# Gate and up products of an FFN in Strassen's seven-product block form, tokens in quarters

## The chip, the cores and the metric

The kernel runs on one core of a Trainium2 chip. The metric is device time in microseconds of one execution. A core has five engines that run their own instruction queues side by side: TensorE (PE, matrix products into PSUM banks), VectorE (DVE), ScalarE (ACT), GpSimd (POOL) and SyncE (SP, which here issues the DMA transfers). They wait for one another through semaphores. The weights of a matmul are loaded by a separate instruction (PEld in the profile) that overlaps the matmul before it.

## The reference

One inference step of one layer for 1,024 prompt tokens and 32 sample tokens (T = 1,056), model width D = 1,024:

```python
proj = x @ w_in                       # 4096 columns: HGRN2 heads and retention heads
o_h, o_r = hgrn2_chunkwise(...), retention_chunkwise(...)   # each head-normalised and gated
x = layer_norm(alpha * x + concat(o_h, o_r) @ w_out)
hidden = silu(x @ w_gate) * (x @ w_up)                      # FF = 2816 columns
x = layer_norm(alpha * x + hidden @ w_down)
```

All of it is in fp32; the outputs are x and the two heads' states. The change concerns the last two lines, with the normalisation ahead of them and the product with `w_out`.

## The kernel before

Features lie on the partitions and tokens along the free axis, so every product is "weights 128x128 times tokens". fp32 accuracy is had by splitting each operand into a rounded part (hi, type fp32r) and the remainder (lo): a product is three matmuls into one PSUM bank, hi·hi, hi·lo and lo·hi (`group`, the matmul in L224). `split` makes the two parts: ACT casts (L187), and DVE or POOL subtracts (L188). `load_w` (L191) has SP fetch a raw 128x1024 tile `wr` (two buffers) and splits it, mostly on POOL, into full hi and lo tiles `wh`/`wl` or `xh`/`xl` (three buffers each).

The order of the work: the program is written as one stream of large products. Beside it stands a queue `side` of generators (normalisation `norm`, mixer steps, centring `center`), and `tick(rate)` after each piece of the stream takes `rate` steps out of it. The tile framework's scheduler then fixes each engine's own order by priorities (`high_priority` moves work ahead).

The phases are: the mixer with the input projection (to about 489 us); the product with `w_out` (`oproj`, L774); and the FFN (L841 on). Tokens come in three chunks of 400, 400 and 256 (`CHB`). `oproj` runs chunk by chunk over eight output tiles m, adding to `Y` (x with its mean over the features taken out: `xload` L757, `xsub` L766 and L768). After each chunk, `norm` squares Y on ACT and adds the squares on DVE and POOL (L685), gets the sum over features and the reciprocal root (`rstd`, matmul L665, Newton steps L213–L217), spreads it over the partitions (`spread`, matmul L656), multiplies Y by it on DVE (L706) and POOL (L704), applies gain and bias on ACT (L707), and splits the result into `X`, the FFN's operand.

The FFN goes through 11 pairs of FF tiles (22 tiles of 128 columns). For each tile and chunk `gu` (L797) makes one full product with `w_gate` and one with `w_up` over all eight k tiles, then silu (ACT, L808), multiplication (DVE, L809) and a split of the hidden tile into `hh` and `hl`. `down` (L812, matmul L822) adds a pair's product with `w_down` into Y on DVE (L834 and L836); the `down` of pair p is issued inside pair p+1, after its first gate and up products, so hidden tiles are long finished by then. In the last pair `down` follows chunk by chunk, and the final `norm` of each chunk with it; `norm_tail` (L736) ends the program. Late in the FFN `center` (POOL, L728 and L733) takes the running mean out of Y, and the last weights of `w_down` are centred.

PSUM has eight banks: in this phase three under the name `pj` and five under `mx`.

Of the kernel before, what the change touches and what calls it, by code (L numbers as in the profile page):

```python
# [9 lines left out]
F32 = mybir.dt.float32  # L10
# [6 lines left out]
P = 128  # L17
# [18 lines left out]
RF = 2.0  # L36
CHB = [(0, 400), (400, 400), (800, 256)]
CBM = 400
# [4 lines left out]
WE = (3, 4, 5)  # L43
TV = (6, 7)
PJ = 3
NH = 5
LP1 = 0
# [16 lines left out]
# columns of the shape-only constants  # L64
# [3 lines left out]
def _consts():  # L68
    parts = []
    off = 0  # L70

    def put(name, a):
        nonlocal off
        a = np.asarray(a, np.float64).reshape(P, -1)
        _CI[name] = (off, a.shape[1])
        off += a.shape[1]
        parts.append(a)
# [29 lines left out]
    cst = np.concatenate(parts, 1).astype(np.float32)  # L107
# [13 lines left out]
    return cst, masks.reshape(P, -1), cs.astype(np.float32)  # L121


_CST, _MASKS, _CS = _consts()


def body(tc, ctx, a):
# [19 lines left out]
    masks = const.tile([P, len(SMALL), 16], U8, name="masks")  # L147
# [4 lines left out]

    def K_(name):
        o, n = _CI[name]
        return cst[:, o:o + n]
# [5 lines left out]
    # work of the mixer and of the norms, woven into the stream of large products  # L161
# [28 lines left out]
    # cen: every row is taken relative to its mean (True) or to the given one  # L190
    def load_w(src, shape=(P, KT, P), ext=None, eng=None, cen=None, keep=None):  # L191
        raw = wp.tile(list(shape), F32, tag="wr", name="wr", bufs=2)
        nc.sync.dma_start(raw, src)
        pool, t = (ext, "x") if ext is not None else (wp, "w")
        hi = pool.tile(list(shape), F32R, tag=t + "h", name=t + "h", bufs=3)
        lo = pool.tile(list(shape), F32R, tag=t + "l", name=t + "l", bufs=3)
        if cen is True:
            mn = tmp.tile([P, 1], F32, tag="mn", name="mn", bufs=2)
            V.tensor_reduce(mn, raw, axis=AX, op=add)
            V.tensor_scalar(mn, mn, -1.0 / shape[1], None, op0=mul)  # L200
            V.tensor_scalar(raw, raw, mn, None, op0=add)
        elif cen is not None:
            V.tensor_tensor(raw, raw, cen.unsqueeze(2).to_broadcast(list(shape)), op=sub)
        split(hi, lo, raw, eng or G)
        if keep is not None:
            keep.append(raw)
        return hi, lo
# [22 lines left out]
    def wk(w):  # L230
        return [(w[0][:, k], w[1][:, k]) for k in range(KT)]
# [4 lines left out]
    # ------------------------------------------------------------ mixer phase  # L236
    with ExitStack() as ctxA:
# [10 lines left out]
        w0 = wp.tile([P, KT, P], F32, tag="wr", name="wr", bufs=2)  # L248
# [392 lines left out]
    with ExitStack() as ctxB:  # L641
# [30 lines left out]
        def norm(c, g, b, final, w1=1, w2=2):  # L672
# [15 lines left out]
            if PS:  # L688
                V.tensor_tensor(s2, s2, sb, op=add)
# [287 lines left out]
```

## Time and profile before

| what | value |
|---|---|
| time of three runs | 1401.8, 1403.86, 1405.06 us (median 1403.86) |
| span of the profiled execution | 1400.3 us |
| PE busy | 97% |
| DVE, ACT, POOL busy | 46%, 27%, 31% |
| HBM traffic | 61 GB/s over the span |

The profile is of one execution. Its span is the time from the first to the last recorded instruction; the times of the runs contain a little more at both ends. In a row of a group the columns are line, engine, operation, output<-inputs, shapes and count, then busy time and mean ns of one, then idle time ahead of them and what ended it. In a row of a timeline they are start, duration, engine, line and names. In a row of windows they are the stretch, its length and then for each engine busy time and count (PE, PEld, DVE, ACT, POOL), the granted PE clock, the share of DMA and GB/s.

### The profile page before, as it was taken

The page shows a single profiled execution, that of the slowest core. Times are in us where ns is not written, and L with a number is a line of the kernel's source. Part 1 is how long each engine was busy: PE and PEld are TensorE (multiplying, and loading weights), DVE is VectorE, ACT ScalarE, POOL GpSimd, SP SyncE. Part 2 cuts the span into 40 slices and gives each one's busy share as a digit, 9 for nine tenths or more (in the row PEclk, how much of TensorE's full clock was granted, in tenths as well). Part 3 has the DMA queues.
Part 4 walks back from the last instruction along what each step waited for, and adds up shares of the span by engine and source line. Part 5 has one row for each costly group of instructions (what it writes and reads, how often), then busy time and mean ns, then how long its engine had stood idle before and what let it go on. Part 6 is the DMA issues. An engine that isn't in the chain of part 4 may idle for free.

```text
span 1400.3 us, 24598 instructions
## 1 busy us (share of the span) xinstructions
PE 1363.5 (97%) x10532; PEld 1337.2 (95%) x10532; DVE 650.8 (46%) x1338; ACT 372.9 (27%) x696; POOL 438.9 (31%) x309
## 2 busy tenths in 40 slices
PE   8999999999999987999999999999999999999996
PEld 7999999999999977999999999999999999999996
DVE  6254253666678759573323232323232325253446
ACT  6333332223322422454020202020202121212035
POOL 2333322121212397564030303030303036813221
PEclk9999999999999998999999999999999999999998
DMA  7212113112151151021110102020202020202002
GB/s 251 75 48 79 48 33 104 34 34 69 57 169 61 48 184 61 15 91 37 40 61 31 63 29 68 23 75 17 76 15 76 16 75 16 76 15 76 16 21 105
DMA packets 46557, 87.11 MB, mean 62 GB/s; under 512 B 3952, under 2 KB 30832, under 8 KB 46448
## 3 DMA queue, kind: packets, MB, share of 16 engines
q1 hardware_dynamic: 46448, 85.54, 18.8%
q8 instruction: 83, 1.36, 0.4%
q14 instruction: 26, 0.21, 0.1%
HBM read 76.48 MB, written 9.04 MB: 61 GB/s over the span
## 4 chain that ended last, share of the span: by engine, by line
PE 90%; DVE 5%; issue 2%; DMA 1%; POOL 1%; ACT 1%; SPq 0%; ACTq 0%; DVEq 0%; POOLq 0%
PE mx L224 36%; PE pj L224 28%; PE pj L822 17%; PE mx L407 1%; PE mx L550 1%; DVE Y L768 1%; PE mx L520 1%; PE mx L822 1%; PE mx L552 1%; DVE s L685 1%; DVE X L188 1%; DMA Y<-in_xT 1%; PE mx L502 1%; DVE Y L766 1%; PE mx L462 1%
## 5 line engine op out<-in xcount | busy, mean ns | idle before, releaser
L224 PE MATMUL mx<-X,wh 128*128 128x400 f32 (+1 forms) x1920 | 455.9, 323 | 0.0
L188 POOL TENSOR_TENSOR wl<-wr,wh 128x1024 fp32r<-128x1024 f32 x78 | 188.3, 2416 | 631.2 <-ACT wh L187 605.9
L224 PE MATMUL pj<-X,wh 128*128 128x352 f32 (+2 forms) x1392 | 343.4, 328 | 5.6 <-ACT X L187 4.9
L224 PEld LDWEIGHTS mx<-X,wh 128*128 128x128 f32 x1920 | 334.8, 188 | 0.5
L224 PE MATMUL mx<-X,wl 128*128 128x400 f32 (+1 forms) x960 | 308.8, 322 | 0.0
L224 PEld LDWEIGHTS pj<-X,wh 128*128 128x128 f32 x1392 | 242.1, 189 | 9.5 <-ACT X L187 4.9
L224 PE MATMUL pj<-X,wl 128*128 128x352 f32 (+2 forms) x696 | 227.8, 327 | 0.9 <-DVE wl L188 0.4
L836 DVE TENSOR_TENSOR Y<-Y,pj 128x400 f32<-128x400 f32 (+1 forms) x225 | 116.4, 520 | 169.6 <-PE pj L822 167.7
L224 PEld LDWEIGHTS mx<-X,wl 128*128 128x128 f32 x960 | 180.2, 188 | 0.2
L822 PE MATMUL pj<-hl,xh 128*128 128x400 f32 (+1 forms) x489 | 157.8, 323 | 0.0
L822 PE MATMUL pj<-hh,xl 128*128 128x400 f32 (+1 forms) x489 | 157.7, 323 | 0.0
L822 PE MATMUL pj<-hh,xh 128*128 128x400 f32 (+1 forms) x489 | 156.9, 323 | 0.0
L809 DVE TENSOR_TENSOR sg<-sg,mx 128x400 f32<-128x400 f32 (+1 forms) x66 | 34.4, 520 | 246.8 <-PE mx L224 246.8
L224 PEld LDWEIGHTS pj<-X,wl 128*128 128x128 f32 x696 | 131.4, 189 | 2.6 <-POOL wl L188 1.1
L187 ACT CAST wh<-wr 128x1024 fp32r<-128x1024 f32 (+1 forms) x83 | 86.3, 1040 | 177.4 <-PE mx L224 74.5
L188 POOL TENSOR_TENSOR xl<-wr,xh 128x1024 fp32r<-128x1024 f32 x28 | 67.3, 2404 | 91.2 <-ACT xh L187 91.1
L187 ACT CAST hh<-sg 128x400 fp32r<-128x400 f32 (+1 forms) x66 | 32.0, 485 | 229.1 <-DVE sg L809 229.1
L822 PEld LDWEIGHTS pj<-hl,xh 128*128 128x128 f32 x489 | 91.9, 188 | 0.1
L822 PEld LDWEIGHTS pj<-hh,xl 128*128 128x128 f32 x489 | 92.0, 188 | 0.0
L822 PEld LDWEIGHTS pj<-hh,xh 128*128 128x128 f32 x489 | 91.9, 188 | 0.0
L224 PE MATMUL pj<-wh,X 128*128 128x256 f32 x512 | 91.4, 280 | 0.0
L808 ACT ACTIVATE sg<-mx 128x400 f32<-128x400 f32 (+1 forms) x66 | 30.6, 463 | 214.5 <-PE mx L224 214.4
(203 smaller groups left out, 1752.1 us busy)
## 6 DMA issues: line engine op xcount, KB each, us to landing
wr<-in_w_in SPq DMA_DIRECT2D x23, 512.0 KB, 3.6
wr<-in_w_gate SPq DMA_DIRECT2D x22, 512.0 KB, 3.5
wr<-in_w_up SPq DMA_DIRECT2D x22, 512.0 KB, 3.5
wr<-in_w_down SPq DMA_DIRECT2D x22, 512.0 KB, 3.5
wr<-in_w_out SPq DMA_DIRECT2D x12, 512.0 KB, 3.5
M<-in_xT SPq DMA_DIRECT2D x24, 176.0 KB, 4.3
wr<-in_w_v SPq DMA_DIRECT2D x8, 512.0 KB, 4.1
wr<-in_w_or SPq DMA_DIRECT2D x8, 512.0 KB, 3.5
```

What stands on the lines that cost most here:

```text
L187: S.copy(hi, src)
L188: (eng or V).tensor_tensor(lo, src, hi.bitcast(F32), op=sub)
L224: PE.matmul(out, l, r, start=(i == 0), stop=(i == n - 1))
L407: PE.matmul(into(B32 * b, (c % 4) * w), k[:, o:o + B32], cols(q, o), start=True, stop=True)
L462: PE.matmul(a_ps[:, c * C:(c + 1) * C], k[:, cc], q[:, cc], start=True, stop=True)
L502: PE.transpose(t_ps[:, c * C:(c + 1) * C], k[:, (4 * b + c) * C:(4 * b + c + 1) * C], ident)
L520: PE.matmul(d_ps[:, c * P:(c + 1) * P], tk[:, 4 * b + c], v[:, 4 * b + c], start=True, stop=True)
L550: PE.matmul(o[:, c * P:(c + 1) * P], at[:, cc], v[:, cc], start=True, stop=(cc == 0))
L808: S.activation(sg, po[0], AF.Silu)
L809: V.tensor_tensor(sg, sg, po[1], op=mul)
L822: PE.matmul(outs[m], wd[i][w][:, ms], hs[c][h][:, i], start=(i == 0 and n == 0), stop=(i == 1 and n == 2))
L836: V.tensor_tensor(y, y, outs[m], op=add)
```

## The change

What it does:

- **Token quarters.** Chunks become four quarters of 264 tokens (`CQ`). `oproj` runs per pair of quarters, over m upwards and then downwards, and loads 14 weight tiles where it loaded 12.
- **Strassen form.** In `unit` a pair of FF tiles, the two halves of the features (k tiles 0–3 and 4–7) and a pair of quarters make a 2x2 by 2x2 block product, done with seven block products (`A11·B11`, `S2·T2`, `S3·T3`, `S1·T1`, `A12·B21`, `A22·T4`, `S4·B22`) where the direct form has eight. Each is 4 k tiles x 3 matmuls of 264 columns. The partial sums are kept in PSUM and in fp32 tiles `u`, `v`; one ACT copy and further DVE additions put them together (L852 to L860, L882, L892).
- **Weight blocks.** `blocks` loads the two raw tiles of a pair and makes seven half tiles (128x512) with four combinations on POOL (L820, L821, L822, L827). Hi and lo half tiles live in one ring `bh`/`bl` of seven buffers each, for all weights; raw tiles have three buffers.
- **Token blocks.** `combine(pr)` makes T1 to T4 (into X) and B11, B21, B22 (into a new tile `XB`) from the normalised Y; `norm` no longer splits into X.
- **Down.** `down` (matmul L908) follows its own pair directly, in quarters 0, 2, 1, 3; nothing of the next pair lies in between.
- **First and last pair** run once per pair of quarters, and so load and make their gate, up and down blocks twice.
- All eight PSUM banks are `mx` in this phase; `tick` rates are 1.0 and, in the first pair, 1.5, where they were 2.0; centring is in two steps, `total` and `center`, after pairs 7 and 8; the last quarter alone goes through `norm_tail`; constants stand in two tiles, and two of the mixer's tables move to a pool that ends with the mixer.

The three places below show how the engines' orders change.

POOL, before, between the end of `oproj` and the first pair (L188 makes lo parts of weights `wl`/`xl` and of X, L685 adds squares, L704 multiplies by the reciprocal root):

```order
L188 TENSOR_TENSOR wl<-wr,wh 128x1024
L188 TENSOR_TENSOR xl<-wr,xh 128x1024
L704 TENSOR_TENSOR Y<-Y,mus 128x400 x4
L188 TENSOR_TENSOR wl<-wr,wh 128x1024
L188 TENSOR_TENSOR xl<-wr,xh 128x1024
L188 TENSOR_TENSOR X<-Y,X 128x400 x4
L188 TENSOR_TENSOR xl<-wr,xh 128x1024
```

POOL, after, in the first pair: up blocks of the first pair of quarters (L193 is the lo part, L820 to L827 the combinations) with the normalisation (L709, L727) and token blocks (XB) of the second pair of quarters:

```order
L820 TENSOR_TENSOR s_7622<-wr 128x512
L709 TENSOR_TENSOR s_7689<-s_7689,q_7691 128x264
L821 TENSOR_TENSOR wr<-wr 128x512
L709 TENSOR_TENSOR s_7689<-s_7689,q_7709 128x264
L822 TENSOR_TENSOR wr<-s_7622,wr 128x512
L193 TENSOR_TENSOR bl<-wr,bh 128x512 x2
L193 TENSOR_TENSOR bl<-s_7622,bh 128x512
L193 TENSOR_TENSOR bl<-wr,bh 128x512 x2
L727 TENSOR_TENSOR Y<-Y,mus 128x264 x4
L193 TENSOR_TENSOR XB<-Y,XB 128x264
L827 TENSOR_TENSOR wr<-wr 128x512
L193 TENSOR_TENSOR XB<-Y,XB 128x264 x7
```

Where one weight tile was one POOL instruction, it is two halves here, with the combinations added, and the token blocks' lo parts stand between them.

DVE, before, in a middle pair: a chunk's multiplication (L809) and lo part (L188) stand among the additions of `down` of the pair before:

```order
L809 TENSOR_TENSOR sg_9904<-sg_9904,mx 128x400
L188 TENSOR_TENSOR hl<-sg_9904,hh 128x400
L836 TENSOR_TENSOR Y<-Y,pj 128x400
L836 TENSOR_TENSOR Y<-Y,pj 128x256 x8
L809 TENSOR_TENSOR sg_9961<-sg_9961,mx 128x256
L188 TENSOR_TENSOR hl<-sg_9961,hh 128x256
L809 TENSOR_TENSOR sg_10028<-sg_10028,mx 128x400
L188 TENSOR_TENSOR hl<-sg_10028,hh 128x400
```

DVE, after, at the end of the up unit of a middle pair: the last partial sums (L892), multiplications (L893) and lo parts (L193) come in one run, and the additions of this same pair's `down` (L915) right behind them:

```order
L892 TENSOR_TENSOR u<-mx,u 128x264
L193 TENSOR_TENSOR h<-u,h 128x264
L893 TENSOR_TENSOR u<-u,h 128x264
L892 TENSOR_TENSOR u<-mx,u 128x264
L193 TENSOR_TENSOR h<-u,h 128x264
L893 TENSOR_TENSOR u<-u,h 128x264
L915 TENSOR_TENSOR Y<-Y,mx 128x264 x2
L193 TENSOR_TENSOR h<-u,h 128x264
L915 TENSOR_TENSOR Y<-Y,mx 128x264 x30
L855 TENSOR_TENSOR u<-mx,u 128x264 x2
```

The hidden tiles that `down` reads are now made just ahead of it.

POOL, before, at the end of the program:

```order
L188 TENSOR_TENSOR hl<-sg_13081,hh 128x400
L704 TENSOR_TENSOR Y<-Y,mus 128x400 x4
L685 TENSOR_TENSOR s_13191<-s_13191,q_13193 128x400
L685 TENSOR_TENSOR s_13191<-s_13191,q_13208 128x400
L188 TENSOR_TENSOR hl<-sg_13218,hh 128x256
L704 TENSOR_TENSOR Y<-Y,mus 128x400 x4
```

POOL, after, at the end of the program:

```order
L193 TENSOR_TENSOR bl<-s_16450,bh 128x512
L193 TENSOR_TENSOR bl<-wr,bh 128x512 x2
L727 TENSOR_TENSOR Y<-Y,mus 128x264 x4
L827 TENSOR_TENSOR wr<-wr 128x512
L193 TENSOR_TENSOR bl<-wr,bh 128x512 x5
L709 TENSOR_TENSOR s_16880<-s_16880,q_16882 128x264
L709 TENSOR_TENSOR s_16880<-s_16880,q_16885 128x264
L727 TENSOR_TENSOR Y<-Y,mus 128x264 x8
```

Weight blocks of the last up unit and of the last `down` now stand between the normalisation steps, and eight multiplications of two quarters end the queue.

The diff, cut to its core:

```diff
-RF = 2.0
-CHB = [(0, 400), (400, 400), (800, 256)]
+RF = 1.0
+RB = 1.5
+CQ = T // 4
+CHB = [(i * CQ, CQ) for i in range(4)]
+RING = 7
...
+    def ring():
+        return [wp.tile([P, HK * P], F32R, tag=t, name=t, bufs=RING) for t in ("bh", "bl")]
+
+    def load_raw(src, shape=(P, KT, P)):
+        raw = wp.tile(list(shape), F32, tag="wr", name="wr", bufs=3)
         nc.sync.dma_start(raw, src)
...
+    def block(src, eng=None):
+        hi, lo = [t.rearrange("p (k n) -> p k n", n=src.shape[2]) for t in ring()]
+        split(hi, lo, src, eng or G)
+        return hi, lo
...
-                else:
-                    split(X[:, 0, m, sl], X[:, 1, m, sl], y, G if m % 2 else V)
...
+        def combine(pr):
+            s0, s1 = qs_(2 * pr), qs_(2 * pr + 1)
+            yield
+            for k in range(HK):
+                i, o = divmod(k, 2)
+                y11, y12, y21, y22 = Y[:, k, s0], Y[:, k, s1], Y[:, HK + k, s0], Y[:, HK + k, s1]
+
+                def put(f, j, src, eng=None):
+                    split(f(j, 0, pr, i)[:, o], f(j, 1, pr, i)[:, o], src, eng)
+
+                t3, t2 = ut(), ut()
+                put(xb, 0, y11, G)
+                V.tensor_tensor(t3, y22, y12, op=sub)
+                V.tensor_tensor(t2, t3, y11, op=add)
+                put(xt, 1, t2)
+                put(xt, 2, t3, G)
+                yield
+                t1, t4 = ut(), ut()
+                V.tensor_tensor(t1, y12, y11, op=sub)
+                put(xt, 0, t1)
+                put(xb, 1, y21, G)
+                V.tensor_tensor(t4, y21, t2, op=sub)
+                put(xt, 3, t4)
+                put(xb, 2, y22, G)
+                yield
+
+        def blocks(src, c, eng=None):
+            E = eng or G
+            w1, w2 = load_raw(src[c]), load_raw(src[c + 1])
+            a11, a12, a21, a22 = w1[:, :HK], w1[:, HK:], w2[:, :HK], w2[:, HK:]
+            out = {"A11": block(a11, eng)}
+            f1 = wp.tile([P, HK, P], F32, tag="s1", name="s1", bufs=1)
+            E.tensor_tensor(f1, a21, a22, op=add)
+            E.tensor_tensor(a21, a11, a21, op=sub)
+            E.tensor_tensor(a11, f1, a11, op=sub)
+            out["S2"] = block(a11, eng)
+            out["S3"] = block(a21, eng)
+            out["S1"] = block(f1, eng)
+            out["A12"] = block(a12, eng)
+            E.tensor_tensor(a12, a12, a11, op=sub)
+            out["A22"] = block(a22, eng)
+            out["S4"] = block(a12, eng)
+            return out
+
+        def unit(w, prs, fin, rate):
...
+            def product(wn, xn, bank, first):
+                for pr in prs:
+                    if first:
+                        bank[pr] = mx()[:, :CQ]
...
+                    for k in range(HK):
+                        for l, r in ((hi, 0), (hi, 1), (lo, 0)):
+                            PE.matmul(bank[pr], l[:, k], rs[k][r], start=(first and n == 0), stop=(n == 3 * HK - 1), skip_group_check=not first)
...
+            for pr in product("A11", "B11", X_, True):
...
+                    S.copy(u[pr], X_[pr])
+            for pr in product("S2", "T2", Y_, True):
...
+                    V.tensor_tensor(u[pr], Y_[pr], u[pr], op=add)
...
+            for pr in product("S1", "T1", Z_, True):
...
+                    fin(1, 1, pr, Z_[pr], v[pr])
+            for pr in product("A12", "B21", X_, False):
...
+                    fin(0, 0, pr, X_[pr], None)
...
+        def up_fin(h):
+            def fin(i, j, pr, ps, u):
+                g, f = h[i, 2 * pr + j], ut()
+                if u is None:
+                    V.tensor_tensor(f, ps, g, op=mul)
+                else:
+                    V.tensor_tensor(f, ps, u, op=add)
+                    V.tensor_tensor(f, f, g, op=mul)
+                h[i, 2 * pr + j] = hi, lo = hid(F32R), hid(F32R)
+                split(hi, lo, f)
+            return fin
...
         for p in range(NPAIR):
...
+            h = {}
+            ends = p in (0, NPAIR - 1)
+            rate = RB if p == 0 else RF
+            for prs in ((0,), (1,)) if ends else ((0, 1),):
+                if p == 0:
+                    drain(("cb", prs[0]))
+                unit(blocks(a["w_gate"], 2 * p), prs, gate_fin(h), rate)
+                unit(blocks(a["w_up"], 2 * p), prs, up_fin(h), rate)
+                qs = [2 * pr + j for j in range(2) for pr in prs]
...
+                if p < NPAIR - 1:
+                    down(wdown(p), h, qs, p == 0, rate / 2)
+                elif prs[0] == 0:
+                    down(wdown(p), h, qs, False, rate / 2)
+                    for q in qs:
+                        side.append((("n2", q), norm(q, l2g, l2b, True, *(W2 if q else (1, 2)))))
+                else:
+                    wd = wdown(p)
+                    down(wd, h, [2], False, rate / 2)
+                    side.append((("n2", 2), norm(2, l2g, l2b, True, 1, 1)))
...
+                    down(wd, h, [3], False, rate / 2, squares)
...
+                    norm_tail(3, parts, l2g, l2b)
```

More of the change, by code (lines that the diff above doesn't have):

```diff
@@ L42 @@
 SG = (1, 3, 5, 7)
-WE = (3, 4, 5)
 TV = (6, 7)
@@ L46 @@
 NH = 5
+HK = KT // 2
 LP1 = 0
@@ new lines, in down @@
+        def down(wd, h, qs, first, rate, squares=None):
+            for j in range(2):
+                for q in qs:
+                    for mm in range(HK):
+                        m = HK * j + mm
+                        out = mx()[:, :CQ]
+                        n = 0
+                        for i in range(2):
+                            hi, lo = wd[i][j]
+                            for w, x in ((hi, 0), (hi, 1), (lo, 0)):
+                                PE.matmul(out, w[:, mm], h[i, q][x], start=(n == 0), stop=(n == 5))
+                                n += 1
+                        y = Y[:, m, qs_(q)]
+                        with tc.high_priority(offset=HP):
+                            if first:
+                                V.scalar_tensor_tensor(y, y, ALPHA, out, op0=mul, op1=add)
+                            else:
+                                V.tensor_tensor(y, y, out, op=add)
+                            if squares is not None:
+                                squares(m, y)
+                        tick(rate)
@@ L790, in oproj @@
-            if c < NC3 - 1:
-                xsub(c + 1, zx[c + 1])
-            side.append((("n1", c), norm(c, l1g, l1b, False)))
-        for c in range(NC3):
-            oproj(c, list(range(KT))[::1 - 2 * (c % 2)])
-        def gu(i, wg, wu, c, hs, mid=None, eng=None):
-            po = []
-            for w in (wg, wu):
-                out = mx()[:, :CHB[c][1]]
-                group(out, wk(w), xk(*CHB[c]), RF)
-                po.append(out)
-                if mid and w is wg:
-                    mid()
-            sg = tt("sg2", CHB[c][1])
-            hh, hl = hs[c]
-            with tc.high_priority(offset=HP):
-                S.activation(sg, po[0], AF.Silu)
-                V.tensor_tensor(sg, sg, po[1], op=mul)
-                split(hh[:, i], hl[:, i], sg, eng)
@@ L812, in down @@
[L812 to L839 removed]
+                    wo[m] = load_w(a["w_out"][m], cen=wbar)
@@ new lines, in oproj @@
+                    wo.pop(m - 2 if pr == 0 else m + 2, None)
+                if pr == 0:
+                    for q in (2, 3):
+                        xload(q, i)
+                for q in qs:
+                    out = mx()[:, :CQ]
+                    group(out, wk(wo[m]), xk(q * CQ, CQ), RO)
+                    y = Y[:, m, qs_(q)]
+                    V.scalar_tensor_tensor(y, y, ALPHA, out, op0=mul, op1=add)
+                    if pr == 0 and i == XS:
+                        xsub(q, ms[:i + 1])
@@ new lines, in oproj, with wdown @@
+            if pr == 0:
+                for q in (2, 3):
+                    xsub(q)
+            for q in qs:
+                side.append((("n1", q), norm(q, l1g, l1b, False)))
+            side.append((("cb", pr), combine(pr)))
+        for m in range(KT):
+            for q in range(2):
+                xload(q, m)
+        for pr in range(2):
+            oproj(pr)
+        def wdown(p):
+            return [load_w(a["w_down"][2 * p + i].rearrange("p (k n) -> p k n", n=P), cen=p > PC or None) for i in range(2)]
```

287 lines of the change are left out of this document (125 added, 162 removed).

## The prediction

> **What bounds the kernel now.** The page first: the busy shares, then the chain that ended last.
>
> ```profile
> PE 1363.5 (97%) x10532; PEld 1337.2 (95%) x10532; DVE 650.8 (46%) x1338; ACT 372.9 (27%) x696; POOL 438.9 (31%) x309
> PE 90%; DVE 5%; issue 2%; DMA 1%; POOL 1%; ACT 1%; SPq 0%; ACTq 0%; DVEq 0%; POOLq 0%
> ```
>
> PE is the chain. Columns taken from it shorten the time, as long as the others keep up. Whether they do differs by stage, so the windows come next: one middle FFN pair, then two stretches of the product with `w_out`.
>
> ```profile
> 878.36:947.84 69.48, 69.48 (x434) 69.45 (x433) 20.96 (x36) 11.70 (x18) 14.54 (x7) 1.00 0.14 46
> 500.00:520.00 20.00, 14.44 (x70) 13.77 (x68) 8.94 (x8) 4.20 (x4) 18.51 (x13) 0.91 0.84 294
> 540.00:560.00 20.00, 12.60 (x59) 11.90 (x58) 19.39 (x27) 3.89 (x6) 11.17 (x7) 0.81 0.17 53
> ```
>
> In the middle pair PE is busy for all 69.48 us, and DVE, ACT and POOL for 20.96, 11.70 and 14.54. Around the normalisation it is the other way round: POOL has 18.51 of 20 us, then DVE 19.39, and PE waits. So the middle pairs will give what the columns say, and the stage from `w_out` to the first pair decides what remains of it.
>
> **The price of a column.** The PE timeline has a group of 48 matmuls of 256 columns and then one of 48 of 400.
>
> ```profile
> 1002.70 0.40 PE L224 MATMUL mx<-X,wh 128*128 128x256 f32 x2
> ...
> 1008.31 0.53 PE L224 MATMUL mx<-X,wh 128*128 128x400 f32 x2
> ...
> 1017.02 0.35 PE L822 MATMUL pj<-hh,xh 128*128 128x400 f32 x1
> ```
>
> 5.61 us over 48 is 116.9 ns; 8.71 over 48 is 181.5 ns. That makes 0.449 ns a column and 2.1 ns a matmul, so 264 columns cost 120.5 ns.
>
> **A middle pair** had 432 matmuls in 69.48 us. It now has gate and up of 7 products x 2 quarter pairs x 12 = 168 matmuls each, and 8 x 4 x 6 = 192 of `down`: 528 x 0.1205 = 63.6 us, 5.9 less. There are nine of them: 53 us. The cover: DVE has 54 additions or evictions that read PSUM (0.43 each by the 256-wide row below) and 14 operations with both inputs in SBUF (about 1 each beside POOL), 37 us in all; POOL has 26 half-tile operations, 34 us; ACT some 20. All lie under 63.6.
>
> **POOL's prices** come from its groups and one piece of its timeline.
>
> ```profile
> L188 POOL TENSOR_TENSOR wl<-wr,wh 128x1024 fp32r<-128x1024 f32 x78 | 188.3, 2416 | 631.2 <-ACT wh L187 605.9 <-issue 13.3 <-PE mx L520 12.0
> L733 POOL TENSOR_TENSOR Y<-Y,mc 128x400 f32<-128x400 f32 x16 | 16.5, 1073 | 0.0
> L733 POOL TENSOR_TENSOR Y<-Y,mc 128x256 f32<-128x256 f32 x8 | 5.8, 764 | 0.0
> L757 POOL TENSOR_TENSOR zs<-zs,Y 128x256 f32<-128x256 f32 x6 | 6.1, 1012 | 0.2
> L728 POOL TENSOR_TENSOR zs<-zs,Y 128x256 f32<-128x256 f32 x6 | 4.5, 754 | 0.3
> 521.97 2.41 POOL L188 TENSOR_TENSOR wl<-wr,wh 128x1024 fp32r<-128x1024 f32 x1
> 524.32 3.07 POOL L757 TENSOR_TENSOR zs<-zs,Y 128x400 f32<-128x400 f32 x2
> ```
>
> Between 256 (764 ns) and 1024 columns (2416) lies a line of 2.15 ns a column: 1.31 us for a half tile, 0.78 for a quarter. The timeline starts the next operation 2.35 after one of 2.41, so in a row they cost 1.26 and 0.73. The same sum on 256 columns takes 1012 ns in the busy stage (L757) and 754 in the quiet one (L728): a collision with DVE costs POOL about 0.25. DVE loses more:
>
> ```profile
> L836 DVE TENSOR_TENSOR Y<-Y,pj 128x256 f32<-128x256 f32 x75 | 31.5, 421 | 44.5 <-PE pj L822 43.4
> L188 DVE TENSOR_TENSOR hl<-sg,hh 128x256 fp32r<-128x256 f32 x21 | 32.0, 1523 | 13.9 <-ACT hh L187 13.9
> 531.22 7.75 DVE L766 SCALAR_TENSOR_TENSOR Y<-mc,Y 128x400 f32<-128x400 f32 x7
> ```
>
> An operation that reads PSUM takes 421 ns; one of the same width with both inputs in SBUF 1523 beside POOL's 2.4 us operations, and 1.1 for 400 columns beside 1.07 us ones.
>
> **From `w_out` to the end of the first pair.** PE's timeline gives the starts of both stages.
>
> ```profile
> 489.38 0.53 PE L224 MATMUL pj<-X,wh 128*128 128x400 f32 x2
> 613.19 0.53 PE L224 MATMUL mx<-X,wh 128*128 128x400 f32 x2
> 1384.62 0.28 PE L822 MATMUL mx<-hh,xl 128*128 128x256 f32 x1
> ```
>
> The last matmul ends at 1384.7; ten pairs of 69.48 before it, pair 0 ends in the same sense at 689.9. I take 489.4 for the mixer's end as it is; its splits in halves cost POOL 0.1 more a half, under PE's cover.
>
> Now: the first 16 groups of `oproj`, 24 matmuls each, take 46.3 us and 3.5 of stalls, to 539. The means that the centring needs come at about 529.5 (as in the trace, where L766 starts at 531); 28 DVE operations with SBUF inputs at 1.1 last until 560. The sums for the normalisation stand behind them on DVE, and PE's matmuls for the reciprocal root behind a finished part of `oproj`: PE waits some 11 us. Newton's steps and the spread take 12 (its longest wait before was 4.5, the rest is groups that stand ahead), and POOL's first multiplication of quarter 0 can start at 575. The trace shows such waits already:
>
> ```profile
> PE mx L665 <- DVE s L689: 10.2, 3, 6.7
> PE mx L656 <- DVE rs L217: 5.6, 2, 4.5
> ```
>
> The last ten groups (2.9 each) and 2 of stalls end `oproj` at 603, where PE alone would then end pair 0 at 603 + 63.6 = 667. But POOL's queue from that multiplication to the last `down` block of pair 0 holds, as its order shows, 57 half-tile operations (18 blocks and 8 combinations, made once for each pair of quarters, 52, and five blocks left of `w_out`) and 52 of a quarter for the normalisation and the token blocks: 57 x 1.26 + 52 x 0.73 = 110 us. DVE has some 80 SBUF operations there; four in five collide, an estimate from POOL being always at work: 16 us. Four times POOL must wait for the cast of a combination that it has just made (0.8: the 617 ns of a half tile and a hand-over), and twice the second raw tile of the up weights gets its buffer only when the gate's last block is made, and lands 3.5 us later under 1.3 of other work: 3.2 + 4.4.
>
> ```profile
> L187 ACT CAST wh<-wr 128x512 fp32r<-128x512 f32 x2 | 1.2, 617 | 2.0 <-DMA wr<-in_w_in 2.0
> wr<-in_w_gate SPq DMA_DIRECT2D x22, 512.0 KB, 3.5
> ```
>
> 575 + 110 + 16 + 8 = 709; behind the last block remain 10 us of `down` (both quarters' second half, 5.8, and 4.5 of the first): pair 0 ends at **719**, 29 later than now. Bounds: 678 if the normalisation's chain is not late and collisions cost nothing, 745 if POOL also waits for quarter 2's normalisation, which stands between its up blocks.
>
> **Hand-over in a middle pair.** `down` now reads what its own pair's up unit has just made. The split of quarter 0 needs the A22 product, 4.3 us before the up unit's end, and eight SBUF operations d of DVE queued from 10.15 before it: ready at -10.15 + 2.6 + 8d. Late from d = 0.94 on, and behind a late split wait all of `down` and the DVE additions. POOL works in half of the time there, so d lies between 0.42 and 1.5; I take 0.9 to 1, 0.5 us a pair (bounds 0 and 4.1). Nine pairs: 9 x 64.1 = 577. Centring two quarters in each of two pairs, 2.
>
> **Last pair and tail.** POOL's 52 half tiles and 8 quarter operations are 71.3, with gaps as above 79; about 14 (eleven operations) can be made during the pair before, and 10 of `down` follow the last block: 75 (bounds 66, 82), against 69.48. The tail is 15.6 us now.
>
> ```profile
> 1386.64 5.00 ACT L707 ACTIVATE Y<-Y,par 128x400 f32<-128x400 f32 x8 [0.32 <-DVE Y L706]
> 1393.65 3.06 ACT L744 ACTIVATE Y<-Y,par 128x256 f32<-128x256 f32 x6 [2.00 <-DVE Y L742]
> ```
>
> Fourteen ACT steps are left after the last matmul; then 22 (three quarters less the two that DVE does), 8 more at 0.6: 20.6 (bounds 15.6, 26).
>
> **Sum**: 719 + 577 + 2 + 75 + 20.6 = 1393.6 against a span of 1400.3. The median of the runs is 3.6 above this span, so **1397 us**.
>
> **Rivals.**
>
> *POOL's work is hidden for the most part.* If the 28 operations of DVE run at 0.57 (the PSUM price for 400 columns is 570) for want of POOL beside them, the chain ends 15 earlier, and if collisions cost POOL nothing, 16 more: 1366. For it: POOL rests at times while DVE works (11.17 of 20 us at 540). Against: the seven operations at 531 took 1.1 each.
>
> *DVE and POOL shut each other out.* Every one of the 80 collides and costs POOL a whole DVE operation, 0.42: +18 in pair 0, +5 in the last: 1420. For it: 1523 ns is 421 and nearly half of POOL's 2416. Against: L757 lost only 0.26, and not at each operation. [...]
>
> *The hand-over is late in every middle pair*: the place is DVE's queue at the end of the up unit, the price 4.1 - 0.5 us nine times at d = 1.45, and it decides from d = 0.94: 1397 + 32 = 1429, slower than before. For it: 1523 at 256 columns. Against: POOL's operations are half as long now and come in bursts.
>
> *No net change*: the 53 us are given back by ends, tail and hand-over in full, 1404.
>
> Ruled out: that a 264-column matmul is held by its weight load; rows of 256 go at 117 ns with the same loads.
>
> **Chances.** Forecast 0.42 (alone 1381 to 1414), hidden 0.20, shut out 0.15, hand-over 0.13, no net change 0.10. A difference under 0.2% (1401.1 to 1406.7 is "same") can't be told from none here. Below 1401: 0.25 of the forecast's, 0.19 of the hidden case's, and 0.06 of the rest, 0.50; within, 0.15; above, 0.35. The range reaches into both side cases, 1363 to 1423.
>
> **What would show it.** Middle pairs of 63.6 to 64.5 us with PE without idle time: the columns right; L908 waiting for h: the hand-over. PE waiting in pair 0 and pair 10 for `bl` (L193) with POOL busy nearly throughout: POOL's queue right; pair 0 ending near 719, the last matmul near 1373. Wrong, if POOL is idle for long in pair 0, if PE waits there for DVE or ACT instead, or if middle pairs exceed 66.

## The result and the profile after

The changed kernel took 1452.24 us (median of 4; 1451.02 to 1453.21) against 1402.87 us of the kernel before on the same chip (1401.8 to 1405.06): ratio 1.0351, 95% interval 1.0337 to 1.0366. It is 3.5% slower. The forecast was 1397 us with a range up to 1423, so the sign and the range were both wrong; the dearest of the four rivals was 1429. The profiled execution of the changed kernel has a span of 1450.8 us, 50.5 more than the one before.

The page after, busy shares and the granted PE clock in 40 slices:

```profile
PE 1340.8 (92%) x11828; PEld 1310.9 (90%) x11828; DVE 826.6 (57%) x1814; ACT 489.1 (34%) x1076; POOL 743.8 (51%) x678
...
PEclk9999999999999898987899999999999998989986
```

PE does less work and is no longer busy throughout: 92% where it was 97%, and its clock dips where the work is not dense. Where this happens is shown by the windows, cut at the stages. The first three are of the kernel before (product with `w_out`, first pair, tail), the six others of the changed kernel (the same two, a middle pair, pair 8, last pair, tail).

```profile
489.40:613.20 123.80, 107.73 (x617) 104.80 (x616) 83.41 (x111) 42.14 (x76) 88.33 (x63) 0.92 0.26 87
613.20:689.90 76.70, 75.87 (x456) 75.51 (x455) 32.43 (x52) 27.64 (x52) 30.91 (x20) 1.00 0.17 56
...
1384.70:1400.30 15.60, 3.48 (x24) 3.02 (x23) 9.50 (x28) 9.28 (x17) 4.00 (x4) 0.63 0.50 172
```

```profile
499.00:620.00 121.00, 106.35 (x801) 105.43 (x802) 84.51 (x132) 39.29 (x88) 84.40 (x87) 0.90 0.26 81
620.00:731.00 111.00, 82.61 (x555) 79.40 (x554) 75.76 (x147) 55.22 (x125) 94.52 (x84) 0.83 0.17 57
...
795.20:859.40 64.20, 64.20 (x530) 64.20 (x529) 31.09 (x68) 18.11 (x39) 34.13 (x26) 1.00 0.16 50
...
1180.50:1258.80 78.30, 67.95 (x534) 67.47 (x533) 42.59 (x74) 18.44 (x41) 55.22 (x56) 0.91 0.13 41
...
1337.20:1421.10 83.90, 73.55 (x544) 70.83 (x543) 57.95 (x110) 38.11 (x88) 64.05 (x53) 0.94 0.22 70
1421.10:1450.80 29.70, 10.05 (x49) 9.68 (x47) 16.45 (x62) 13.90 (x29) 5.70 (x8) 0.56 0.32 109
```

Set beside the prediction's sum, stage by stage (us):

| stage | before | predicted | after |
|---|---|---|---|
| start of the product with `w_out` | 489.4 | 489.4 | 498.9 |
| product with `w_out` | 123.8 | 113.6 | 121.1 |
| first pair | 76.7 | 116 | 111.0 |
| nine middle pairs, without centring | 625.3 | 577 | 577.8 |
| centring, in pairs 8 and 9 | (in the pairs) | 2 | 28.4 |
| last pair | 69.5 | 75 | 83.9 |
| tail | 15.6 | 20.6 | 29.7 |
| span | 1400.3 | 1393.6 | 1450.8 |

The seven undisturbed middle pairs take 64.2 us each, 5.3 less than before, with PE busy for all of it: the saving is there. It is given back by the product with `w_out`, by the two end pairs, by two places that the forecast took for free or nearly so (the start of the `w_out` product and the centring), and by the tail. PE's waits in the changed kernel, in the order of their sums, name them:

```profile
PE mx L681 <- DVE rs L233: 30.9, 6, 7.6
PE mx L738 <- POOL u L750: 20.7, 2, 10.4
PE mx L844 <- ACT bh L192: 15.3, 7, 6.2
PE mx L240 <- DVE sg L390: 8.7, 1, 8.7
PE mx L844 <- DVE u L860: 5.1, 3, 2.5
...
PE mx L908 <- DVE h L193: 4.1, 4, 2.9
```

L681 spreads the reciprocal root, L738 is the mean for the centring, `bh` is a weight block's hi part. The hand-over (L908 for `h`) is small, and none of it lies in pairs 1 to 7: 3.8 of the 4.1 us are in the first pair.

**The centring.** This is POOL's timeline in pair 8, and PE's beside it:

```profile
1201.48 0.76 POOL L750 TENSOR_TENSOR u<-Y 128x264 f32<-128x264 f32 x1
1202.19 5.76 POOL L758 TENSOR_TENSOR Y<-Y,u 128x264 f32<-128x264 f32 x8
1207.87 0.77 POOL L750 TENSOR_TENSOR u<-u,Y 128x264 f32<-128x264 f32 x1
1208.57 3.73 POOL L193 TENSOR_TENSOR bl<-wr,bh 128x512 fp32r<-128x512 f32 x3
1212.23 3.55 POOL L750 TENSOR_TENSOR u<-u,Y 128x264 f32<-128x264 f32 x4
1215.74 1.26 POOL L820 TENSOR_TENSOR s<-wr 128x512 f32<-128x512 f32 x1
1216.95 0.74 POOL L750 TENSOR_TENSOR u<-u,Y 128x264 f32<-128x264 f32 x1
```

```profile
1207.12 0.28 PE L844 MATMUL mx<-XB,bl 128*128 128x264 f32 x1
1217.75 1.25 PE L738 MATMUL mx<-u,cst 128*128 128x264 f32 x2 [10.35 <-POOL u L750]
...
1219.45 0.64 PE L844 MATMUL mx<-X,bh 128*128 128x264 f32 x2
1219.89 0.42 PE L844 MATMUL mx<-X,bl 128*128 128x264 f32 x1
```

The seven sums of the second quarter begin at 1201.5, and then the eight subtractions of the first quarter's centring (5.76 us) and three weight blocks (3.73) go ahead of most of the rest, and one combination (L820) ahead of the last. The mean's matmul stands at a fixed place in PE's queue, and 10.35 us pass there with nothing done, twice (pairs 8 and 9).

**The clock after a wait.** In the last two rows two matmuls of 264 columns start 0.44 us apart: 0.22 each, not 0.12. The windows of two such stretches, which begin in the waits of 8.67 and of 10.35 us:

```profile
492.80:503.00 10.20, 4.15 (x19) 4.15 (x20) 7.62 (x10) 3.20 (x9) 7.44 (x7) 0.50 0.66 208
1209.60:1223.20 13.60, 5.45 (x23) 5.24 (x24) 4.38 (x2) 0.38 (x1) 12.79 (x16) 0.50 0.24 77
```

The granted clock is 0.50 there. Counted over the whole trace there are 14 such stretches ahead of the last product, of 3.4, 6.8, 10.2 or 13.7 us, each beginning during a wait of 2 us or more or within 2.7 us of its end, with 253 product matmuls in them at 0.10 us more each: 25 us. The kernel before had three, with 27 product matmuls of 400 columns and 27 of 256, some 7 us. In these two kernels the shortest wait with such a stretch behind it was 2.03 us, yet 2 us is no limit: the kernel before has a wait of 2.09 us with none behind it. Counted over all fourteen traces, from 15 us on and ahead of the last product, each of the 78 waits of 3.5 us or more has a stretch that begins in it or within 4 us of its end, and so have 45 of the 60 between 2 and 3.5 us and 11 of the 72 between 1 and 2.

### The profile page after: what moved, and what is told of

Same layout as the page of the kernel before. It is cut to its first block, busy times and chain, and to the rows that moved or that the text cites. A ratio compares the mean times of both kernels' runs of the same rounds, so it can differ in the third digit from the quotient of the medians.

```text
span 1450.8 us, 28884 instructions
## 1 busy us (share of the span) xinstructions
PE 1340.8 (92%) x11828; PEld 1310.9 (90%) x11828; DVE 826.6 (57%) x1814; ACT 489.1 (34%) x1076; POOL 743.8 (51%) x678
## 5 line engine op out<-in xcount | busy, mean ns | idle before, releaser
L193 POOL TENSOR_TENSOR bl<-wr,bh 128x512 fp32r<-128x512 f32 x292 | 387.4, 1338 | 428.5 <-ACT bh L192 387.9
L192 ACT CAST bh<-wr 128x512 fp32r<-128x512 f32 x300 | 180.8, 619 | 337.4 <-PE mx L908 96.4
L240 PE MATMUL pj<-X,bh 128*128 128x352 f32 (+1 forms) x1168 | 285.9, 326 | 6.3 <-ACT X L192 4.5
L844 PE MATMUL mx<-X,bh 128*128 128x264 f32 x1408 | 270.2, 293 | 16.8 <-ACT bh L192 11.6
L908 PE MATMUL mx<-h,bh 128*128 128x264 f32 x1408 | 261.0, 288 | 8.3 <-DVE h L193 4.1
L844 PEld LDWEIGHTS mx<-X,bh 128*128 128x128 f32 x1408 | 226.3, 196 | 18.7 <-ACT bh L192 12.5
L908 PEld LDWEIGHTS mx<-h,bh 128*128 128x128 f32 x1408 | 220.3, 191 | 10.2 <-DVE h L193 5.9
L240 PEld LDWEIGHTS pj<-X,bh 128*128 128x128 f32 x1168 | 201.3, 189 | 9.3 <-ACT X L192 4.5
L844 PE MATMUL mx<-X,bl 128*128 128x264 f32 x704 | 203.4, 291 | 1.0 <-POOL bl L193 1.0
L844 PE MATMUL mx<-XB,bh 128*128 128x264 f32 x1056 | 200.3, 289 | 4.3 <-ACT bh L192 3.6
L908 PE MATMUL mx<-h,bl 128*128 128x264 f32 x704 | 197.0, 286 | 0.2 <-POOL bl L193 0.2
L915 DVE TENSOR_TENSOR Y<-Y,mx 128x264 f32<-128x264 f32 x320 | 130.5, 426 | 64.5 <-PE mx L908 63.7
L908 PEld LDWEIGHTS mx<-h,bl 128*128 128x128 f32 x704 | 132.3, 190 | 0.4 <-POOL bl L193 0.4
L240 PE MATMUL mx<-X,bh 128*128 128x264 f32 x512 | 102.3, 300 | 8.7 <-DVE sg L390 8.7
L240 PEld LDWEIGHTS mx<-X,bh 128*128 128x128 f32 x512 | 85.2, 201 | 9.1 <-DVE sg L390 8.9
```

The lines of the kernel that those rows point to most:

```text
L192: S.copy(hi, src)
L193: (eng or V).tensor_tensor(lo, src, hi.bitcast(F32), op=sub)
L240: PE.matmul(out, l, r, start=(i == 0), stop=(i == n - 1))
L844: PE.matmul(bank[pr], l[:, k], rs[k][r], start=(first and n == 0), stop=(n == 3 * HK - 1), skip_group_check=not first)
L908: PE.matmul(out, w[:, mm], h[i, q][x], start=(n == 0), stop=(n == 5))
L915: V.tensor_tensor(y, y, out, op=add)
```

## The experiments

The first four change one thing in the changed kernel. The next four stand on the first (sums on DVE). A difference in a stage is read from the trace of each; the whole times of these eight are single executions, beside 1402.0 and 1402.5 us for the kernel before.

**1. The running sums of the centring on DVE.**

```diff
-                G.tensor_tensor(zs, Y[:, 0, qs_(q)] if m == 1 else zs, Y[:, m, qs_(q)], op=add)
+                V.tensor_tensor(zs, Y[:, 0, qs_(q)] if m == 1 else zs, Y[:, m, qs_(q)], op=add)
```

> Edit: in the centring after pairs 7 and 8, the running sums over the features (L750) go from POOL to DVE; nothing else. In the changed kernel pairs 8 and 9 take 78.2 and 78.2 us where the others take 64.2, and PE waits 10.35 us in each for L750, whose last sums stand on POOL behind 8 centring subtractions and three weight blocks. Theory (POOL's queue makes the sum late): the waits at L738 go, pairs 8 and 9 come down to 64 to 66 us, the whole by 25 to 28 us, to about 1425. [...]

Measured: 1427.1 us, 25 less. The window of pair 8:

```profile
1181.30:1247.00 65.70, 65.37 (x535) 65.05 (x534) 51.16 (x88) 18.00 (x41) 48.51 (x42) 1.00 0.14 49
```

65.7 us, no wait at L738, clock 1.00. POOL's order was the cause. The sums are dear on DVE too (1047 ns each, where POOL took 778 in the changed kernel), but nothing waits for them there. 1.5 us a pair remain, 3 in all where the prediction allowed 2.

**2. Another PSUM bank for the first group of `w_out`: banks only named.**

```diff
+        for _ in range(PJ):
+            mx()
```

> Edit: three PSUM banks are taken and left ahead of the product with w_out, so that its first group falls on the fourth bank and not on the one that the mixer's last gating step still reads. In the changed kernel PE waits 8.67 us there for DVE (L390) and the clock is granted at half for 10.2 us after it. Theory (the wait is for a bank, by the new sharing of all eight): the wait shrinks to under 2 us, the product starts near 490 and the time falls by 8 to 11 us. Rival (the wait only shows that the operands X are not ready: their last splits end at 498 to 501): the wait stays at 6 us or more under another name, and nothing is gained.

Measured: 1450.6 us, and the same 8.7 us of waiting for L390. Three tiles that nothing writes seem to hold no bank, so the edit did not do what it was for; it is no evidence for either side. Experiment 5 repeats it properly.

**3. PE kept busy where the sum is late.**

```diff
+            for _ in range(fill):
+                PE.matmul(mu, X[:, 0, 0, 0:P], X[:, 0, 0, :CQ], start=True, stop=True)
             PE.matmul(mu, K_("mean"), zs, start=True, stop=True)
...
-            mcs[q] = mean(zs)
+            mcs[q] = mean(zs, 84 if q % 2 else 0)
```

> Edit: 84 extra matmuls of 264 columns, whose result is overwritten, stand on PE some 25 product matmuls ahead of each late mean (pairs 8 and 9); 84 x 0.1205 = 10.1 us of work that nothing needs. Theory (idle time of 2 us or more brings a stretch of half clock, in which a 264-column matmul takes 0.22 us): the 10.35 us of idle time become 10.1 of work, the half-clock stretches of 13.7 us in these pairs go, and each pair gets 2 to 4 us faster, 74 to 76 us, in spite of the extra work. Rival (the half clock has its own reason, such as the power of the whole chip at that time): the stretches stay and the pairs take 78 us or more.

Measured: 1447.8 us. The extra matmuls on PE, and the window of pair 8:

```profile
1204.94 10.36 PE L739 MATMUL mx<-X 128*128 128x264 f32 x84
```

```profile
1181.10:1256.40 75.30, 75.30 (x618) 75.17 (x617) 43.61 (x74) 18.81 (x41) 56.77 (x56) 1.00 0.12 43
```

Ten microseconds of useless work in place of 10.35 of waiting make the pair 3.0 us shorter (75.3 for 78.3), and the clock stays at 1.00. Pair 9 takes 75.3 as well. So in these two waits the idle time itself brings the half clock, and it is paid a second time; for the shorter waits this is concluded from the place of their stretches alone.

**4. No lo parts of weights in the end pairs.** The hi block stands in the place of the lo block, so PE has the same matmuls, and the output leaves out the lo·hi products of these two pairs.

```diff
+        if skip[0]:
+            S.copy(hi, src)
+            return hi, hi
         split(hi, lo, src, eng or G)
...
+            skip[0] = ends
```

> Edit: in the first and last pair POOL makes no lo parts of weights; the hi block is used in their place, so the output leaves out the products lo x hi of these two pairs (replaced by hi x hi) and PE has the same matmuls. This takes 36 of the 52 half-tile operations from POOL in each of the two pairs (47 us of 68). Theory of the prediction (POOL's queue sets the length of the end pairs): the first pair falls from 111.3 us to under 90, the last from 83.8 to 68 to 72. Rival (the chain of the normalisation, DVE sums, Newton's steps and the matmuls for it that stand in PE's order, sets them): under 8 us less in the first pair, the waits of L681 for rs and of L844 for u stay. The tail after the last matmul of the products stays near 29.7 by both.

Measured: 1419.9 us. The windows of the first and the last pair:

```profile
620.50:711.90 91.40, 74.40 (x555) 72.09 (x554) 66.21 (x143) 53.72 (x124) 50.74 (x50) 0.93 0.20 70
1317.70:1389.30 71.60, 68.20 (x545) 67.52 (x543) 47.35 (x111) 38.50 (x88) 23.61 (x22) 0.98 0.24 82
```

The first pair falls from 111.0 to 91.4 and the last from 83.9 to 71.6, the tail stays at 28.7. The lo parts of weights on POOL are 20 of the 47 us by which the first pair exceeds 63.6, and 12 of the 20 of the last. The first pair just misses the "under 90" of the theory. Of its other 27.8 us, 11.2 are the rival's, PE's waits for the reciprocal root (38.2 us over the whole run, the largest sum by far), with two stretches at half clock of 6.8 us behind them.

**5. Another bank, taken by a write.**

```diff
+        for _ in range(PJ):
+            V.memset(mx()[:, :1], 0.0)
```

> Edit, on top of the sums on DVE (1427.1 us): a one-column DVE write takes three PSUM banks ahead of the product with w_out, so that the first group is really on another bank; in the run before, the three banks that were only named were given back at once and the same bank was waited for. Theory (the wait of 8.7 us for L390 is for the bank): it goes, and with it a half-clock stretch of 10.2 us, 1418 to 1420. Rival (the operands are late): PE waits 6 us or more for X or for Y, time within 3 us of 1427.

Measured: 1424.0 us, 3 less than experiment 1. The wait is gone and the product starts at 490.2, 9.1 earlier: it was the bank. But the first pair starts only 6 us earlier, since the product takes 3 longer (among it a new wait of 4.0 us at L738 for the sums of x, L929, on POOL), and as the two end pairs and the tail also grow, 3 us reach the end. The 7 to 9 that were expected did not come; the time lies between the theory and the rival, and the waits are as the theory has them.

**6. The spread of the first normalisation later in PE's queue.**

```diff
-                side.append((("n1", q), norm(q, l1g, l1b, False)))
+                side.append((("n1", q), norm(q, l1g, l1b, False, 1, 8)))
```

> Edit, on top of the sums on DVE: in the first normalisation the matmuls that spread the reciprocal root (L681) come six steps later in the stream than before, behind more product matmuls. In the run with the sums on DVE, PE waits 18.5 us in three places for Newton's steps (L233) between 560 and 640, each with a half-clock stretch after it. Theory (they stand too early in PE's order, and what waits for the normalised quarters has slack): 10 to 20 us less, 1408 to 1417. Rival (the normalised quarters themselves are on the path, so that later is later): the waits change their name to bh, h or u in the first pair, and the time stays within 5 us or grows.

Measured: 1431.2 us, 4 more than experiment 1. The windows of the `w_out` product and the first pair:

```profile
499.30:611.10 111.80, 104.01 (x802) 103.13 (x803) 77.03 (x115) 36.62 (x80) 82.61 (x84) 0.95 0.27 89
611.00:735.20 124.20, 87.79 (x553) 81.24 (x553) 93.35 (x164) 57.95 (x133) 97.68 (x87) 0.79 0.15 51
```

Beside experiment 1 the product is 9.8 us shorter and the first pair 13.2 longer, where PE now waits for X (L193 and L192, 20.9 us). The rival was right: the normalised quarters are on the path, and moving PE's wait only renames it.

**7. The gate and up blocks of the end pairs on DVE.**

```diff
+                eng = V if ends else None
-                unit(blocks(a["w_gate"], 2 * p), prs, gate_fin(h), rate)
-                unit(blocks(a["w_up"], 2 * p), prs, up_fin(h), rate)
+                unit(blocks(a["w_gate"], 2 * p, eng), prs, gate_fin(h), rate)
+                unit(blocks(a["w_up"], 2 * p, eng), prs, up_fin(h), rate)
```

> Edit, on top of the sums on DVE: in the first and last pair the gate and up blocks (combinations and lo parts, 22 half-tile operations per pair of quarters) are made on DVE, POOL keeps those of down. The run without lo parts gave 19.8 and 12.2 us in the two pairs for 47 us of POOL work taken away. A half tile should take DVE some 0.6 us (1024 columns took 1.22 where DVE did them) against 1.29 on POOL. Theory (POOL's queue is the limit, DVE has room): first pair 111 to 90-98, last 83.6 to 72-78, in all 15 to 30 us less. Rival (DVE, busy 65 to 99% there, is as full as POOL): within 8 us of 1427, or slower, with PE waiting for u, h and sums on DVE.

Measured: 1413.5 us, 13.6 less. First and last pair, and PE's largest wait:

```profile
619.80:721.10 101.30, 77.39 (x554) 73.84 (x553) 83.16 (x183) 52.72 (x121) 47.70 (x45) 0.88 0.19 63
1302.80:1382.30 79.50, 69.07 (x544) 68.24 (x543) 67.50 (x146) 39.07 (x88) 19.01 (x18) 0.94 0.22 74
```

```profile
PE mx L681 <- DVE rs L233: 47.9, 8, 9.1
```

POOL is down from 94.5 to 47.7 us in the first pair, and almost no wait for `bh` is left (0.3 us); DVE makes a lo part of a half tile in 0.70 where POOL needs 1.3. The pairs fall by 9.7 and 4.2, a half and a third of what taking the lo parts away altogether gave, short of the 90 to 98 and 72 to 78; the whole gain lies between theory and rival. What remains is mainly the normalisation's chain, with longer waits now (17.6 us in the first pair where it was 6.3), presumably because DVE also has the blocks.

**8. Twice the side work per product in the last pair.**

```diff
-            rate = RB if p == 0 else RF
+            rate = RB if p == 0 else (2.0 if ends else RF)
```

> Edit, on top of the sums on DVE: in the last pair the stream takes two steps of the side work per product where it took one (before the change it took two). The tail after the last product is 29.0 us and holds the normalisation of three quarters, since the steps of quarter 1 run out of stream to hide in. Theory: quarter 1 is done under the products, the tail falls to 20 to 23 us and the last pair grows by at most 4: 1420 to 1424. Rival (the steps only crowd POOL and DVE in the last pair): the last pair grows by what the tail loses, within 3 us of 1427.

Measured: 1424.7 us, 2.4 less. Last pair and tail:

```profile
1312.50:1402.60 90.10, 76.39 (x560) 73.88 (x558) 66.47 (x135) 43.32 (x100) 66.69 (x57) 0.92 0.23 78
1402.60:1422.90 20.30, 6.77 (x31) 6.54 (x30) 9.62 (x37) 7.99 (x16) 2.85 (x4) 0.55 0.31 107
```

The tail falls by 8.8 to 20.3, as expected, but the last pair grows by 6.4, more than the 4 allowed, and the time is within the rival's 3 us of 1427. Most of what the tail loses is work that is on the path wherever it is put.

**9 and 10. Together.** Experiments 1, 5 and 7, and the spreads later for quarters 2 and 3 of the first normalisation and, in the last pair, for quarter 0; then the same with 8, and the last pair's spreads placed to fit.

```diff
-                side.append((("n1", q), norm(q, l1g, l1b, False)))
+                side.append((("n1", q), norm(q, l1g, l1b, False, 1, 10 if pr else 2)))
```

> Edit: sums on DVE, the three banks taken by a write, the gate and up blocks of the end pairs on DVE (each as tried alone), and, new, the spread matmuls (L681) of quarters 2 and 3 eight steps later in the first pair and those of quarter 0 five steps later in the last. With the blocks on DVE the run stood at 1413.5 us; left in its pairs 0 and 10 were waits of 8.5, 9.1 and 7.7 us of PE for Newton's steps, each with a stretch of half clock. Theory (for quarters 2 and 3 and for the last normalisation there is slack, so there the spread may come later, unlike for quarters 0 and 1, where it cost as much as it gave): those 25 us of waits mostly go, the first pair falls from 101 to 80-86 and the last from 79.5 to 71-75, the banks give 3: 1382 to 1394, faster than before the change. Rival (quarters 2 and 3 are on the path too): the waits turn into waits for X and h as when all four came later, 1405 to 1415.

> Edit: as the run together with it (sums, banks, blocks, later spreads), and two steps of side work per product in the last pair, with its spreads placed for that rate. Alone the rate took 8.8 us from the tail and gave 6.5 to the last pair, of which waits on POOL that the blocks on DVE now relieve. Theory: tail 20 to 21 us, last pair 72 to 78: 4 to 8 us below the other run. Rival: the side work and the blocks crowd DVE in the last pair, and the two runs are within 3 us.

Measured: 1403.27 us (ratio to the kernel before 1.0009, interval 0.9999 to 1.0019) and 1400.52 us (0.9987, 0.9975 to 0.9999). The first pair is 95.2 and 95.8 us, not 80 to 86: of the 18 us of waits for the root in it 1 is left, but 10.5 for X stand in their place. Again the rival was right about the waits, with 6 us of gain in the first pair beside it; the time lies between its range and the theory's. The second version's last pair takes 85.1 us for 77.1 and its tail 21.1 for 29.9, and the two versions are 2.75 us apart: the rival's case, by its "within 3". Neither version differs from the kernel before by more than 0.3%.

**11 and 12. The pace of the side work, and the spread in one piece.** On top of experiment 10, `RB` goes from 1.5 to 2.5, with the numbers of steps ahead of the spreads raised to fit; then `LP2`, the priority of the spread matmuls of both normalisations, from -50 to 500.

```diff
-RB = 1.5
+RB = 2.5
```

```diff
-LP2 = -50
+LP2 = 500
```

> Edit, on top of the version with the rate of the last pair: 2.5 steps of side work per product in the first pair where it took 1.5, with the spreads of quarters 2 and 3 counted out for that. In that version PE waits 7.6 and 2.9 us at the start of the second pair of quarters for the token blocks of quarters 2 and 3 (X), since 46 steps of side work stand against 33 that the stream of the first half pair gives. Theory (the pace of the side work makes these blocks late): the waits go and the first pair falls from 95.8 to 83-90 us, 1388 to 1395 in all. Rival (DVE, POOL and ACT are full in the first half of the pair, so that a quicker pace only changes what PE waits for): first pair 93 to 98, within 4 us of 1400.

> Edit, on top of the run with the pace: the spread matmuls of a quarter (L681) stand together on PE; before, the second of the three stood behind another half group of products. In the run with the end blocks on DVE, DVE stood idle for 4.1 and 5.4 us behind the first of them, waiting for the copy of the spread (L723). Theory (that delay is on the path of the first normalisation): quarters 0 and 1 are ready 5 to 8 us earlier and the product with w_out to the first pair's end is 4 to 8 us shorter, tail unchanged. Rival (PE then waits the longer at the first of them): within 3 us of the other run.

Measured: 1402.19 us (0.9997, 0.9987 to 1.0006) for the pace, first pair 99.6: no gain, the rival's case by its time, though the pair lies above its 93 to 98. With the spread in one piece 1394.77 us (0.9947, 0.9932 to 0.9962). Its windows of the `w_out` product, first pair, last pair and tail:

```profile
490.40:612.90 122.50, 105.09 (x804) 103.52 (x803) 91.78 (x159) 47.15 (x110) 88.13 (x92) 0.92 0.26 88
612.70:710.20 97.50, 77.05 (x555) 73.88 (x554) 80.94 (x177) 51.99 (x118) 50.72 (x45) 0.89 0.19 65
1291.80:1371.90 80.10, 71.71 (x556) 70.47 (x555) 69.65 (x162) 41.24 (x93) 21.62 (x22) 0.96 0.22 75
1371.90:1392.70 20.80, 7.31 (x37) 7.07 (x35) 10.75 (x45) 11.23 (x24) 3.03 (x5) 0.58 0.44 149
```

Up to the first pair's end it is 5.5 us shorter than the run with the pace (710.2 for 715.7), in the size foreseen; the tail is 3.6 shorter as well, which was not, and the last pair 1.8 longer. This version is faster than both kernels, 0.5% below the one before and 4% below the changed one.

## Why the prediction was wrong

By its own steps:

- **The price of a column, and a middle pair**: right in the price, and closer than it deserved. 120.5 ns, 63.6 us and a hand-over of 0.5 gave 64.1; seven pairs took 64.2. But PE was busy throughout and did not wait for `h` there, so no hand-over was paid: a matmul cost 121.6 ns (64.2 us over 528), and that the two small errors cancel is luck. The operations of DVE on which the hand-over hung took 0.70 us on average (L193 for `h`, shown further down), under the 0.94 from which it would be late. The rival of the late hand-over, the dearest of the four, did not happen.
- **"Centring two quarters in each of two pairs, 2"**: this step failed most, 28.4 us, 26 of the 57 by which the sum was short. It was put down without a working, though the change made it a wait of PE: the mean's matmul stands in PE's queue, and its sums stand on POOL behind other work. The order of POOL around L758 and L750 would have shown it. Experiment 1 shows the cause.
- **What a wait costs**: the sum counted the waiting time alone. Each of the 14 waits of 2 us or more between the mixer's end and the last product also brought a stretch at half clock, shown by experiment 3 to be the idle time's doing for the two longest; 25 us in all, some 7 of them in the `w_out` product (68 product matmuls in its stretches), which took 7.5 more than predicted. The kernel before already had it, in the quoted row with the clock at 0.81; it was read as a sign that PE waits, and not as a second price.
- **"I take 489.4 for the mixer's end as it is"**: 9.5 us were lost there, 9.1 of them to a bank. The eight banks under one name begin where the mixer's last gating step still reads. Experiment 5 shows it, and also that only 3 of the 9 reach the end.
- **From the `w_out` product to the first pair's end**: 111 us for the pair where 116 were summed, but not for the reason given, so that this nearness too is luck. The sum made POOL's queue the path, with 126 us of work and 8 of waiting from its first multiplication to the last `down` block. The window over the forecast's stretch shows POOL idle for 29 of 134 us:

```profile
575.00:709.00 134.00, 102.79 (x700) 99.81 (x700) 92.08 (x169) 69.47 (x161) 104.95 (x101) 0.83 0.13 44
```

The 109 operations of that sum took 116 us and had 26 of waiting between them, mostly for casts of ACT and once, 6.0 us, for the spread of the root, and ended at 720.8 in place of 709. The sign that was named for POOL's queue, PE waiting for `bl`, hardly showed (1.5 us in the first pair); PE waited there for ACT's `bh` (10.8 us), for the root (6.3), for `h` on DVE (3.8) and `u` (3.0), which the prediction itself had named as a sign of being wrong. Without 36 of POOL's operations 91.4 us remain (experiment 4). The other part is the normalisation's chain with the half clock behind its waits: placing PE's matmuls for it later or quickening the side work (experiments 6, 9 and 11) only renamed the waits or left the time as it was, while keeping the spread in one piece (experiment 12), which shortens the chain, gave 5.5 us.
- **Collisions, 16 us on POOL**: too much. The 109 operations cost some 6 us above the 110 reckoned for them undisturbed; a half tile took 1.35 us in the first pair on average and 1.26 at the least. DVE pays instead, as the rows below show. The rival in which POOL loses a whole DVE operation (0.42 us) each time falls with it: a half tile lost 0.11.
- **The last pair, 75**: 83.9. POOL's lo parts make 12.3 of the 20.3 above PE's own 63.6 (experiment 4), where the sum had 11 for POOL's whole queue; the rest is left open, the root's waits and the clock among it.
- **The tail, 20.6**: 29.7. The estimate counted ACT's steps. What it left out are three normalisations in a row, each with a wait of PE for Newton's steps on DVE:

```profile
1426.00 0.80 PE L681 MATMUL mx<-cst,rs 128*128 128x128 f32 x2 [4.31 <-DVE rs L233]
...
1432.73 0.79 PE L681 MATMUL mx<-cst,rs 128*128 128x128 f32 x2 [4.01 <-DVE rs L233]
...
1442.07 1.45 PE L681 MATMUL mx<-cst,rs 128*128 128x128 f32 x6 [4.05 <-DVE rs L233]
```

The kernel before had one such wait there, 4.50 us. Eight more ACT steps at 0.5 us, which the sum had, and two more waits of 4, which it had not, make 12 of the 14 us by which the tail grew.

So the direction was lost not by one large term alone but by several places at which work that had stood under PE came to stand ahead of it: the centring (26 us over its term), the mixer's end, the tail and the last pair (9 each) and the half clock in the `w_out` product (7). What stays open is how the first pair's 97.5 us in the best version divide between Newton's chain, ACT and DVE; no run takes one of these away alone.

## What to carry to other kernels

A saving on the busiest engine is read off reliably from its own rows; what it meets at the seams is not, so list every instruction in that engine's queue that waits for another engine, and look at what stands ahead of its source there. Price a wait of 2 us or more with the half clock behind it: in the changed kernel somewhat under 2 us on top on average (25 us over 14 waits). If a wait on the path is moved later and comes back under another name, it is the chain that is long, and only a shorter chain helps.

## What the runs showed of the hardware

DVE and POOL, when both read SBUF: the operations of DVE and of POOL in groups, in the changed kernel (the first row reads PSUM, the second SBUF alone; the third is POOL's).

```profile
L915 DVE TENSOR_TENSOR Y<-Y,mx 128x264 f32<-128x264 f32 x320 | 130.5, 426 | 64.5 <-PE mx L908 63.7
L193 DVE TENSOR_TENSOR h<-u,h 128x264 fp32r<-128x264 f32 x88 | 60.8, 698 | 10.3 <-ACT h L192 6.2
```

```profile
L193 POOL TENSOR_TENSOR bl<-wr,bh 128x512 fp32r<-128x512 f32 x292 | 387.4, 1338 | 428.5 <-ACT bh L192 387.9
```

And one row of DVE's timeline in pair 8:

```profile
1205.01 8.54 DVE L217 TENSOR_SCALAR wr<-wr,mn 128x1024 f32<-128x1024 f32 x1
```

DVE's operation with both inputs in SBUF takes 0.43 us on average where no operation of POOL runs beside it and 0.83 where one does (0.70 over all 88 of the second row); POOL's takes 1.29 with no such operation of DVE beside it and 1.40 with one (1.34 over all 292 of the third). The last row is the extreme: a subtraction that took 0.74 us at the least lasted 8.54 while POOL ran an unbroken row of operations from 1202 to 1213; in pair 9 the same happened, with 8.20. It was not expected that POOL nearly keeps its speed and DVE stands still for so long. The subtraction reads one tensor alone, so two inputs are not its reason; what is, no run shows. Both times it ended 0.55 us after the first gap in POOL's row (of 0.08 and 0.07 us) began. That DVE gets its turn only where such a row breaks is what these two cases suggest; no run tests it, and two others of the eight subtractions took 1.20 and 0.94 us while POOL was busy throughout.
